# A decoder layer on one core: first channel group of two chunks, sixteen grouped blocks, x loaded first

## Chip, cores and metric

The kernel runs on one core of a Trainium2 chip. The metric is the device time of one launch in microseconds (us). Engines are TensorE (PE; PEld its weight load), VectorE (DVE), ScalarE (ACT), GpSimd (POOL), and SyncE (SP), which issues most DMAs.

## The reference, cut to what matters

One layer (256 tokens, D = 2048). A conditioning vector c gives shifts, scales and gates; the normalised x goes through one wide projection whose columns feed three token mixers and their gates; then an output projection and a SwiGLU FFN.

```
mod = silu(c) @ w_ada + b_ada
shift1, scale1, gate1, shift2, scale2, gate2 = split(mod, 6)
h = rms_norm(x, norm1_gain) * (1 + scale1) + shift1
proj = h @ w_in                      # 13840 columns: q, k, v of two attentions and a GLA, r_gla, a_gla, gates
g = sigmoid(gate_cols)               # three branches x 2048 columns, the last 6144 columns
y = g[0] * (o_sb @ w_br_sb) + g[1] * (o_dil @ w_br_dil) + g[2] * (o_gla @ w_br_gla)
x = x + gate1 * (y @ w_out)
h = rms_norm(x, norm2_gain) * (1 + scale2) + shift2
x = x + gate2 * ((silu(h @ w_gate) * (h @ w_up)) @ w_ffn_out)
```

## The kernel before

All matrix products are done on TensorE with each fp32 operand split in a high and a low part (hi, lo). `mm3` issues three products per 128-row chunk of channels, 512-column block and 128-token tile: hi x hi (L170), hi x lo of the weights (L171), lo of the activation x hi (L172). `load_weights` brings two chunks of 512 columns in one DMA into `raw` (4 buffers), ACT casts them into `whi` (L162, 4 buffers) and VectorE subtracts to get `wlo` (L163, 4 buffers). `block` runs the products of one column block over a range of chunks, for both token tiles, into two PSUM banks of the pool `acc` (4 banks).

h needs shift1 and scale1 for each of the 16 channel chunks, and these are sums over all of w_ada's rows, which have to be loaded first. So the first 13 column blocks of w_in (0 to 12) are not run over all 16 chunks at once. The chunks are cut in groups, `GROUPS` = (0 to 3), (3 to 7), (7 to 11), (11 to 16). For each group, `proj_block(g, b)` runs all 13 blocks over the chunks of that group, and between the blocks `ada_group` loads the part of w_ada for the next group and adds it up on VectorE: `ada_mac` (L295 for the first row chunk, L297 for the others), 16 row chunks per piece of at most four channel chunks. At the end of a piece the columns are summed over partitions by transposes (L347) and a reduction (L348), `finish_columns` (L354, L357) adds bias and gain, and `make_h` writes the hi part (L464, ACT), the fp32 value (L470, ACT, or L468, VectorE) and the lo part (L471, VectorE) of h.

The sum of a block over its groups lies in an SBUF tile A0 to A12. In the first group ACT copies the banks there (L508), in the next two VectorE adds the banks to it (L510), both token tiles. In the last group, `LAST`, ACT puts the sum back into PSUM first (L496, a seed), the products go on top of it, and ACT copies the result out (L508). The last block of a group goes on in the next one without leaving PSUM (`carry`).

`first_group` sets the start. SP issues c, three w_ada tiles, one pair of w_in chunks, x in four DMAs, then the other thirteen w_ada tiles. TensorE runs filler products of a constant tile (`keep_warm`, L452; `WARM` gives 22, 38 and 13) around the transposes of the small vectors (L256, L259) and the scaled transposes of x (`norm1`, L445). ACT does the exponential for silu(c) (L227), the squares of x (L422), the diagonal of row factors (L439) and the copies of the transposes (L446). The sums of the first two chunks are columns products with ones (L339), that of the third goes by transposes (L573). Then the first real product follows.

After the grouped blocks come the mixers between the last group's blocks, then the blocks for r_gla and for the gates (`gate_block`, three branches times four column blocks, each over all 16 chunks), the branch products (`y_block`), the output projection and the FFN. In the background, by `tick` at a rate per two chunks (`RATE_IN`, `RATE_MID`), the other segments of w_ada are loaded and added up by VectorE.

The order on each engine is worked out ahead by a scheduler from priorities (`prio`) and readiness; `tc.issue_after` forces an instruction behind another one.

Of the kernel before, what the change touches and what calls it, by code (L numbers as in the profile page):

```python
# [17 lines left out]
P = 128  # L18
# [14 lines left out]
RATE_IN, RATE_MID = 0.8, 0.6  # L33
# [6 lines left out]
WARM = (22, 38, 13)  # L40
FIN = 13
GROUPS = ((0, 3), (3, 7), (7, 11), (11, 16))
# [35 lines left out]
def trunk(ctx: ExitStack, tc: tile.TileContext, I, out):  # L78
# [95 lines left out]
    def block(pss, act, src, k0, k1, c0, base=0, w=None, tiles=range(NT), go_on=False, more=False, seeded=False,  # L174
              steps=None, pace=None):

        if w is None:  # L180
            w = load_weights(src, k0, k1, c0)
        if pace is None:
            pace = 1.0 if tiles[-1] == NT - 1 else 0.0
        for k in range(k0, k1):
            if (k - k0) % 2 == 0:
                tick(state["rate"] * pace)
            if k - k0 == DEFER and later:
                with tc.issue_after(state["mm"].ins), prio():
                    later.pop()()
            if steps and k - k0 in steps:  # L190
                with tc.issue_after(state["mm"].ins), prio():
                    steps[k - k0]()
            wh, wl = w[k - k0]
            for t in tiles:
                h, l = act(base + k, t)
                mm3(pss[t], h, l, wh, wl, k == k0 and not go_on, k == k1 - 1 and not more, seeded)
# [30 lines left out]
    nc.scalar.activation(ctmp, c_ps, AF.Exp, scale=-1.0)  # L227
# [75 lines left out]
    def ada_group(k0, k1, tags=ADA_TAGS, between=None):  # L303

        n = k1 - k0
        sh, sc = mod1[:, 0, k0:k1], mod1[:, 1, k0:k1]
        count = 0
# [28 lines left out]
        gains[GROUPS.index((k0, k1))] = (sh, sc)  # L336
# [78 lines left out]
    def norm1():  # L415
# [3 lines left out]
        for t in range(NT):  # L419
            for hf in range(2):  # L420
                junk = S(f"H{t}", [P, 2, NB])
                act(junk, xin[2 * t + hf], AF.Square, accum_out=part[:, hf, t : t + 1])  # L422
# [36 lines left out]
    def make_h(k, sh, sc, early=False):  # L459

        src = xT[k // 4][:, k % 4, :]
        hf = scr([P, T])
        hi = hT[0][k // 4][:, k % 4, :]
        done = nc.scalar.activation(hi, src, AF.Identity, bias=sh, scale=sc)  # L464
        state.setdefault("h_first", done)
        state["h_hi"] = done
        if early:
            nc.vector.tensor_scalar(hf, src, sc, sh, op0=ALU.mult, op1=ALU.add)  # L468
        else:
            nc.scalar.activation(hf, src, AF.Identity, bias=sh, scale=sc)  # L470
        state["h_lo"] = nc.vector.tensor_tensor(hT[1][k // 4][:, k % 4, :], hf, hi.bitcast(F32), op=ALU.subtract)  # L471
# [14 lines left out]

    def proj_block(g, b, w=None, carry=False, steps=None):
        k0, k1 = GROUPS[g]
        go_on = bool(carried)
        pss = carried.pop() if go_on else [acc_bank() for _ in range(NT)]  # L490
        seeded = g == LAST and not go_on
        if seeded:

            with prio():
                for t in range(NT):
                    nc.scalar.copy(pss[t], A[b][:, t, :])  # L496
            go_on = True
        block(pss, h_at, w_in, k0, k1, b * NB, w=w, go_on=go_on, more=carry, seeded=seeded, steps=steps)
        if carry:
            carried.append(pss)  # L500
            return
        with prio():
            first = A[b] is None
            if first:
                A[b] = S(f"A{b}", [P, NT, NB])
            for t in range(NT):
                if first or seeded:
                    nc.scalar.copy(A[b][:, t, :], pss[t])  # L508
                else:
                    nc.vector.tensor_add(A[b][:, t, :], A[b][:, t, :], pss[t])  # L510

# [10 lines left out]
    def first_group():  # L522
# [4 lines left out]
        tags = tuple(f"A{j}" for j in range(9)) + ADA_TAGS  # L527
        raws = []

        def load(ks):  # L530
            for k in ks:
                raw = S(tags[k % len(tags)], [P, 2, w])
                nc.sync.dma_start(raw, w_ada[k * P : (k + 1) * P, : 2 * D].rearrange("p (s c) -> p s c", s=2)[:, :, :w])
                raws.append(raw)
# [16 lines left out]
        for k in range(KC - 1):  # L551
            with tc.issue_after(split.ins) if k > 3 else nullcontext():
# [3 lines left out]

        def last_mac(q):
            return ada_mac(acc[:, :, chunk(q)], raws[KC - 1][:, :, chunk(q)], KC - 1)

        for q in range(n):  # L560
            last_mac(q)
        behind = state["warm"]
        for q in range(n):
            if q < 2:
                sums = misc_bank([P, 2])
                for j in range(2):
                    with tc.issue_after(behind.ins):
                        behind = column_sum(sums[:, j : j + 1], acc[:, j, chunk(q)])
            else:
                ps = misc_bank([P, 2, P])  # L570
                for j in range(2):
                    with tc.issue_after(behind.ins):
                        behind = nc.tensor.transpose(ps[:, j, :], acc[:, j, chunk(q)], ident)  # L573
                sums = small([P, 2])
                with tc.issue_after(state["h_lo"].ins):
                    nc.vector.reduce_sum(sums, ps, axis=AX.X)
            finish_columns(sums[:, 0:1], sh[:, q : q + 1], SEG_SHIFT1, q)
            finish_columns(sums[:, 1:2], sc[:, q : q + 1], SEG_SCALE1, q, ROW_N1)
            make_h(q, sh[:, q : q + 1], sc[:, q : q + 1], True)
            if q == 1:  # L580
                state["casts_after"] = state["h_hi"].ins
                with tc.issue_after(state["h_lo"].ins):
                    early.extend(load_weights(w_in, 2, n, orders[0][0] * NB, ahead=False))
# [9 lines left out]
    nc.vector.tensor_scalar(qg_sb[:, 0:1], vec[:, ROW_SBQ : ROW_SBQ + 1], rs, None, op0=ALU.mult)  # L593
    nc.vector.tensor_scalar(qg_sb[:, 1:2], vec[:, ROW_DILQ : ROW_DILQ + 1], rs, None, op0=ALU.mult)

    for g in range(len(GROUPS) - 1):
        nxt = ada_group(*GROUPS[g + 1])
        steps = KC * -(-(GROUPS[g + 1][1] - GROUPS[g + 1][0]) // 4)
        done = 0
        for n, b in enumerate(orders[g]):  # L600
            while done < (steps * n // (FIN - 1) if g == 0 else steps * (n + 1) // FIN) and next(nxt, "end") != "end":
# [4 lines left out]
            proj_block(g, b, early if (g, n) == (0, 0) else None, carry=n == 12)  # L606
        for _ in nxt:
            pass
        h_group(g + 1)

# [426 lines left out]
    ring["tags"] = ("AR0", "AR1", "KC", "OD")  # L1037

# [17 lines left out]
    gtags = (("A2", "A3", "A4"), ("A7", "A8", "T0"))  # L1056
    gates = {}

    def gate_block(n, br, steps=None):
# [3 lines left out]
        g = S(gtags[n % 2][br], [P, NT, NB])  # L1063
# [19 lines left out]
    for br in range(3):  # L1083
        nc.scalar.activation(gates[0, br], gates[0, br], AF.Sigmoid)
# [78 lines left out]
    for br in range(3):  # L1163
        gate_block(1, br)
    y_block(0)
    for br in range(3):
        gate_block(2, br)
    y_block(1)
    for br in range(3):
        gate_block(3, br)  # L1170
# [457 lines left out]
```

## Time and profile before

| | before |
|---|---|
| median of 3 runs | 1582.43 us (1582.24 to 1582.99) |
| span of the profiled execution | 1580.9 us (its own time is not given beside the span) |
| TensorE busy | 1570.4 us, 99% |
| VectorE busy | 1346.6 us, 85% |
| ScalarE busy | 856.1 us, 54% |
| DMA, mean over the span | 254 GB/s |
| granted TensorE clock | 1.000 |

The page counts an engine busy from the start to the modelled end of each instruction. The span runs from the first to the last instruction; the median of the runs lies 1.5 us above it. A timeline row gives the start, the busy time, the engine, the line, what is written from what, the shapes and the count; in square brackets stands the idle time before it and what ended it. A row of the groups gives the total busy time in us, the mean of one in ns, and the idle time before the group. A row of the windows gives, after the length, the busy time and count of PE, PEld, DVE, ACT and POOL, the granted clock, the DMA share and GB/s. A row of the waits gives the total in us, how often, and the longest.

### The profile page before, as it was taken

How to read it: one execution, taken by the hardware profiler on the slowest of the kernel's cores; microseconds unless marked ns; L12 is line 12 of the kernel's file. 1: busy time of each engine (PE TensorE's matmuls, PEld its weight loads, DVE VectorE, ACT ScalarE, POOL GpSimd, SP SyncE). 2: the span in 40 equal slices, each digit the busy share in tenths (PEclk: the TensorE clock that was granted, in tenths of full speed). 3: DMA queues.
4: the chain of work that ended last, by engine and by line, in shares of the span. 5: the costliest groups of instructions: out<-in, count | busy, mean ns of one | idle time of the engine just before them, and what ended most of it. 6: DMA issues, size and time to landing. Idle time of an engine off the chain costs nothing.

```text
span 1580.9 us, 20197 instructions
## 1 busy us (share of the span) xinstructions
PE 1570.4 (99%) x7219; PEld 1300.1 (82%) x7219; DVE 1346.6 (85%) x1632; ACT 856.1 (54%) x1186; POOL 12.6 (1%) x24
## 2 busy tenths in 40 slices
PE   8999999999999999999999999999999999999998
PEld 7878888888888888888888888888888888888887
DVE  6889996888888687877777887999999999999986
ACT  5654448875755444444445645555555555455553
POOL 1000000000000000000000000000000000000000
PEclk9999999999999999999999999999999999999999
DMA  9999987677788899889777785665566556876664
GB/s 335 350 336 323 336 301 241 219 227 224 238 280 271 293 318 321 305 273 312 269 267 245 257 299 196 211 211 190 198 200 207 195 198 218 303 236 194 222 211 147
DMA packets 196316, 402.26 MB, mean 254 GB/s; under 512 B 13102, under 2 KB 28116, under 8 KB 196216
## 3 DMA queue, kind: packets, MB, share of 16 engines
q1 hardware_dynamic: 194952, 397.75, 74.8%
q0 software_dynamic: 1088, 3.16, 0.5%
q8 instruction: 57, 0.93, 0.2%
q14 instruction: 43, 0.35, 0.1%
q10 hardware_dynamic: 176, 0.07, 0.0%
HBM read 395.68 MB, written 5.24 MB: 254 GB/s over the span
## 4 chain that ended last, share of the span: by engine, by line
PE 92%; ACT 3%; DVE 2%; DMA 1%; issue 1%; SPq 0%; ACTq 0%; DVEq 0%
PE acc L172 22%; PE acc L171 22%; PE acc L170 22%; PE misc L171 6%; PE misc L170 6%; PE misc L172 6%; DMA raw<-w_in 1%; ACT whi L162 1%; PE acc L452 1%; PE misc L821 1%; PE misc L1135 1%; DVE wlo L163 1%; DMA A<-x 0%; PE misc L445 0%; ACT A L508 0%
## 5 line engine op out<-in xcount | busy, mean ns | idle before, releaser
L162 ACT CAST whi<-raw 128x1024 fp32r<-128x1024 f32 x325 | 329.7, 1018 | 361.2 <-PE acc L172 267.6
L163 DVE TENSOR_TENSOR wlo<-raw,whi 128x1024 fp32r<-128x1024 f32 x325 | 380.5, 1178 | 142.0 <-ACT whi L162 140.7
L170 PE MATMUL acc<-whi,H 128*128 128x512 f32 x1145 | 447.8, 392 | 1.2 <-ACT H L464 0.8
L171 PE MATMUL acc<-wlo,H 128*128 128x512 f32 x1145 | 446.4, 390 | 0.8 <-DVE wlo L163 0.7
L172 PE MATMUL acc<-whi,H 128*128 128x512 f32 x1145 | 446.4, 390 | 0.5 <-DVE H L471 0.4
L172 PEld LDWEIGHTS acc<-whi,H 128*128 128x128 f32 x1145 | 214.8, 188 | 46.2 <-DVE H L471 1.6
L170 PEld LDWEIGHTS acc<-whi,H 128*128 128x128 f32 x1145 | 215.0, 188 | 45.8 <-ACT H L464 1.3
L171 PEld LDWEIGHTS acc<-wlo,H 128*128 128x128 f32 x1145 | 215.1, 188 | 44.9 <-DVE wlo L163 1.7
L1357 ACT CAST whi<-raw 128x1024 fp32r<-128x1024 f32 (+1 forms) x163 | 155.3, 968 | 112.2 <-PE acc L172 39.2
L1343 DVE TENSOR_TENSOR wlo<-raw,whi 128x1024 fp32r<-128x1024 f32 (+1 forms) x163 | 178.1, 1115 | 10.0 <-ACT whi L1357 8.9
L172 PE MATMUL acc<-whi,A 128*128 128x512 f32 x234 | 91.1, 389 | 0.0
L170 PE MATMUL acc<-whi,A 128*128 128x512 f32 x224 | 87.7, 391 | 0.0
L171 PE MATMUL acc<-wlo,A 128*128 128x512 f32 x224 | 87.2, 389 | 0.0
L170 PE MATMUL misc<-whi,H 128*128 128x512 f32 (+1 forms) x201 | 78.2, 389 | 0.0
L171 PE MATMUL misc<-wlo,H 128*128 128x512 f32 (+1 forms) x201 | 78.0, 388 | 0.0
L172 PE MATMUL misc<-whi,H 128*128 128x512 f32 (+1 forms) x201 | 77.9, 388 | 0.0
L1343 DVE TENSOR_TENSOR A<-raw,A 128x1024 fp32r<-128x1024 f32 (+2 forms) x59 | 61.2, 1049 | 5.7 <-ACT A L1357 5.3
L1357 ACT CAST A<-raw 128x1024 fp32r<-128x1024 f32 (+1 forms) x47 | 45.8, 988 | 33.5 <-PE acc L172 14.0
L297 DVE SCALAR_TENSOR_TENSOR ada<-AR,csil,ada 128x1024 f32<-128x1024 f32 x39 | 49.7, 1280 | 6.9 <-DMA AR<-w_ada 6.9
L172 PEld LDWEIGHTS acc<-whi,A 128*128 128x128 f32 x234 | 43.9, 188 | 9.2
L171 PEld LDWEIGHTS acc<-wlo,A 128*128 128x128 f32 x224 | 42.1, 188 | 8.6
L170 PEld LDWEIGHTS acc<-whi,A 128*128 128x128 f32 x224 | 42.1, 188 | 8.5
(501 smaller groups left out, 2488.7 us busy)
## 6 DMA issues: line engine op xcount, KB each, us to landing
raw<-w_in SPq DMA_DIRECT2D x205, 512.0 KB, 5.0
raw<-w_ffn_in SPq DMA_DIRECT2D x176, 512.0 KB, 4.5
raw<-w_ffn_out SPq DMA_DIRECT2D x74, 512.0 KB, 5.2
AR<-w_ada SPq DMA_DIRECT2D x58, 512.0 KB, 5.0
raw<-w_out SPq DMA_DIRECT2D x32, 512.0 KB, 5.0
OS<-w_ada SPq DMA_DIRECT2D x24, 512.0 KB, 6.4
KC<-w_ada SPq DMA_DIRECT2D x23, 512.0 KB, 5.1
KD<-w_ada SPq DMA_DIRECT2D x21, 512.0 KB, 5.5
```

The lines of the kernel that those rows point to most:

```text
L162: state["cast"] = nc.scalar.copy(hi[:, :n, :], raw[:, :n, :])
L163: state["split"] = nc.vector.tensor_tensor(lo[:, :n, :], raw[:, :n, :], hi[:, :n, :].bitcast(F32), op=ALU.subtract)
L170: nc.tensor.matmul(ps, lh, rh, start=start, stop=False, skip_group_check=seeded)
L171: nc.tensor.matmul(ps, lh, rl, start=False, stop=False, skip_group_check=seeded)
L172: state["mm"] = nc.tensor.matmul(ps, ll, rh, start=False, stop=stop, skip_group_check=seeded)
L297: nc.vector.scalar_tensor_tensor(acc, raw, c, acc, op0=ALU.mult, op1=ALU.add)
L452: state["warm"] = nc.tensor.matmul(ps, ones_r, wide, start=True, stop=True)
L821: nc.tensor.matmul(ps[:n, t * N_GLA + h, :].rearrange("p (s l) -> p s l", l=L), at(f, h, t)[:, :n], odd(at(f, h, t)), start=True, stop=True,)
L1135: nc.tensor.transpose(ps[:, i, :], src[:, i * P : (i + 1) * P], ident)
L1343: done = nc.vector.tensor_tensor(dst, x, y, op=ALU.subtract)
L1357: nc.scalar.copy(hi[:, :n, :], src)
```

## The change

The channel groups become five: (0 to 2), (2 to 5), (5 to 8), (8 to 11), (11 to 16). The blocks that run by groups become sixteen: blocks 13 to 15 are the second column block of each gate branch, which ran over all chunks as `gate_block(1, br)` before. Their sums lie in three new tiles A13 to A15, and their sigmoid is done later. Room is made by a smaller scratch for GpSimd's DMA descriptors.

In the groups in the middle the sum of the second token tile is put back into PSUM by ACT and copied out by ACT, as in the last group; that of the first tile is still added by VectorE. In the last group both tiles are put back.

At the start x is loaded before the w_ada tiles; these hold two chunks each and have tiles of their own (A0 to A7, two per tile). The first weight pair is issued behind ten of them. Its cast and the squares of x are tied behind the exponential of c. The fillers are 22, 13 and 10. The modulation sums of all later groups are one sequence, due at steps 16, 37, 58 and 80 by the end of each group. The background rate `RATE_MID` goes from 0.6 to 0.7, and the gate tiles are dealt out anew.

```diff
-RATE_IN, RATE_MID = 0.8, 0.6
+RATE_IN, RATE_MID = 0.8, 0.7
-WARM = (22, 38, 13)
-FIN = 13
-GROUPS = ((0, 3), (3, 7), (7, 11), (11, 16))
+WARM = (22, 13, 10)
+GROUPED = 16
+GROUPS = ((0, 2), (2, 5), (5, 8), (8, 11), (11, 16))
+ADA_BY = (16, 37, 58, 80)
...
-    nc.scalar.activation(ctmp, c_ps, AF.Exp, scale=-1.0)
+    c_exp = nc.scalar.activation(ctmp, c_ps, AF.Exp, scale=-1.0)
...
-                act(junk, xin[2 * t + hf], AF.Square, accum_out=part[:, hf, t : t + 1])
+                with tc.issue_after(c_exp.ins):
+                    act(junk, xin[2 * t + hf], AF.Square, accum_out=part[:, hf, t : t + 1])
...
-    A = [None] * 13
-    up, down = list(range(13)), list(range(12, -1, -1))
-    orders = (up[1:] + up[:1], up, down)
+    A = [None] * GROUPED
+    up, down = list(range(GROUPED)), list(range(GROUPED - 1, -1, -1))
+    orders = (up, down, up, down)
...
+    def column(b):
+        return b * NB if b < 13 else COL_G + (b - 13) * D + NB
...
-        pss = carried.pop() if go_on else [acc_bank() for _ in range(NT)]
-        seeded = g == LAST and not go_on
+        if go_on:
+            pss, held = carried.pop()
+        else:
+            pss = [acc_bank() for _ in range(NT)]
+            held = () if first else (0, 1) if g == LAST else (1,)
             with prio():
-                for t in range(NT):
+                for t in held:
                     nc.scalar.copy(pss[t], A[b][:, t, :])
...
-                if first or seeded:
+                if first or t in held:
                     nc.scalar.copy(A[b][:, t, :], pss[t])
                 else:
                     nc.vector.tensor_add(A[b][:, t, :], A[b][:, t, :], pss[t])
...
-        load(range(0, 3))
-        early.extend(load_weights(w_in, 0, 2, orders[0][0] * NB, ahead=False))
+        load_x()
+        load(range(0, 5))
+        state["casts_after"] = c_exp.ins
+        early.extend(load_weights(w_in, 0, n, column(orders[0][0]), ahead=False))
         split = state["split"]
-        load_x()
-        load(range(3, KC))
+        load(range(5, KC // 2))
...
-            with tc.issue_after(split.ins) if k > 3 else nullcontext():
+            with tc.issue_after(split.ins) if k >= 13 else nullcontext():
                 ada_mac(acc, raws[k], k)
...
+            with tc.issue_after(state["h_f"].ins) if q else nullcontext():
+                finish_columns(sums[:, 0:1], sh[:, q : q + 1], SEG_SHIFT1, q)
+                finish_columns(sums[:, 1:2], sc[:, q : q + 1], SEG_SCALE1, q, ROW_N1)
...
-    nc.vector.tensor_scalar(qg_sb[:, 0:1], vec[:, ROW_SBQ : ROW_SBQ + 1], rs, None, op0=ALU.mult)
+    with tc.issue_after(state["h_lo"].ins):
+        nc.vector.tensor_scalar(qg_sb[:, 0:1], vec[:, ROW_SBQ : ROW_SBQ + 1], rs, None, op0=ALU.mult)
...
+    def ada_groups():
+        for a, b in GROUPS[1:]:
+            yield from ada_group(a, b)
+    nxt, done = ada_groups(), 0
+    for g in range(LAST):
+        base = ADA_BY[g - 1] if g else 0
         for n, b in enumerate(orders[g]):
+            due = ADA_BY[0] * n // (GROUPED - 1) if g == 0 else base + (ADA_BY[g] - base) * (n + 1) // GROUPED
+            while done < due and next(nxt, "end") != "end":
                 done += 1
...
+    for b in range(13, GROUPED):
+        proj_block(LAST, b)
...
-    gtags = (("A2", "A3", "A4"), ("A7", "A8", "T0"))
-    gates = {}
+    gtags = {0: ("A2", "A3", "A4"), 2: ("A7", "A8", "T0"), 3: ("A2", "A3", "A4")}
+    gates = {(1, br): A[13 + br] for br in range(3)}
...
-    for br in range(3):
-        gate_block(1, br)
...
-    nc = _bacc.Bacc("TRN2", target_bir_lowering=False, num_devices=1)
+    nc = _bacc.Bacc("TRN2", target_bir_lowering=False, num_devices=1, dynamic_dma_scratch_size=4096)
```

More of the change, by code (lines that the diff above doesn't have):

```diff
@@ L195, in block @@
                 h, l = act(base + k, t)
-                mm3(pss[t], h, l, wh, wl, k == k0 and not go_on, k == k1 - 1 and not more, seeded)
+                mm3(pss[t], h, l, wh, wl, k == k0 and not (go_on or t in held), k == k1 - 1 and not more, seeded or t in held)
     def split_from_psum(hi, lo, ps):
@@ L306, in ada_group @@
         sh, sc = mod1[:, 0, k0:k1], mod1[:, 1, k0:k1]
+        gains[GROUPS.index((k0, k1))] = (sh, sc)
         count = 0
```

79 lines of the change are left out of this document (30 added, 49 removed).

## The prediction

> **What bounds the kernel now.** I read the page first (span, busy shares, the chain that ended last), then what TensorE waits for, then the start of the timeline.
>
> ```profile
> span 1580.9 us, 20197 instructions
> ...
> PE 1570.4 (99%) x7219; PEld 1300.1 (82%) x7219; DVE 1346.6 (85%) x1632; ACT 856.1 (54%) x1186; POOL 12.6 (1%) x24
> ...
> PE 92%; ACT 3%; DVE 2%; DMA 1%; issue 1%; SPq 0%; ACTq 0%; DVEq 0%
> ```
>
> ```profile
> PE acc L171 <- DVE wlo L163: 0.7, 1, 0.7
> PE acc L172 <- DVE H L471: 0.4, 1, 0.4
> ```
>
> The reader is to see that TensorE holds 92% of the chain and, once real work runs, waits for almost nothing: these two are the longest of its waits on VectorE. Shortening any other engine inside the span is worth nothing unless it ends one of these waits. What can be won lies where TensorE is busy with work that computes nothing, and that is the start:
>
> ```profile
> 2.71 7.43 PE L452 MATMUL acc<-H,ones_r 128*128 128x512 f32 x22
> 9.41 1.05 ACT L162 CAST whi<-raw 128x1024 fp32r<-128x1024 f32 x1 [5.97 <-DMA raw<-w_in]
> 10.37 0.18 ACT L227 ACTIVATE tiny<-misc 128x16 f32<-128x16 f32 x1
> 10.72 1.06 ACT L422 ACTIVATE H<-A 128x1024 f32<-128x1024 f32 x1 [0.17 <-DMA A<-x]
> 10.84 0.24 PE L256 MATMUL misc<-ident,H 58*128 58x58 f32 x1 [0.69 <-DMA A<-x]
> 11.09 9.12 PE L452 MATMUL acc<-H,ones_r 128*128 128x512 f32 x38
> 18.49 0.69 ACT L439 ACTIVATE H<-ident,tiny 128x128 f32<-128x128 f32 x2
> 20.05 7.31 PE L445 MATMUL misc<-H,A 128*128 128x128 f32 x64
> 27.11 3.28 PE L452 MATMUL acc<-H,ones_r 128*128 128x512 f32 x13
> 29.00 1.28 DVE L297 SCALAR_TENSOR_TENSOR ada<-A,csil,ada 128x256 f32<-128x256 f32 x3
> 30.23 0.95 PE L339 MATMUL misc<-ones_r,ada 128*128 128x1 f32 x8
> 32.25 0.50 PE L170 MATMUL acc<-whi,H 128*128 128x512 f32 x1 [0.80 <-ACT H L464]
> ```
>
> L452 is filler (22 + 38 + 13 matmuls of one constant tile). The first product with weights comes at 32.25 us. Before it stand the chain x, squares (L422), diagonal (L439), the 64 scaled transposes (L445), and beside it the modulation sums on VectorE (L297), whose last piece ends at 30.3, just as the last filler does. From 32.25 on, the time is the matmul count times its pace.
>
> **The change, part by part.**
>
> *Matmul count.* The grouped blocks do 16 x 16 chunk products instead of 13 x 16, and the three gate blocks that did the other 3 x 16 later are gone. The transposes that sum the modulation columns stay at 28 (two chunks go by the ones product, fourteen by transposes; before, two and fourteen as well). So TensorE's real work is equal; only filler goes, 73 to 45.
>
> *The start, by TensorE.* The 38 fillers took 20.05 - 11.09 = 8.96 us, 0.236 each; 25 fewer is 5.9. The 13 took 30.23 - 27.11 = 3.12, 0.24 each; 3 fewer is 0.7. Together 6.6 us, if what they cover is ready that much earlier: the diagonal at about 13.5 to 14.2 and the sums at about 23.6.
>
> *The start, by DMA.*
>
> ```profile
> 0.00:10.00 10.00, 7.47 (x23) 5.76 (x23) 0.75 (x5) 1.87 (x2) 4.26 (x13) 1.00 0.79 255
> 10.00:20.00 10.00, 9.31 (x41) 7.45 (x41) 8.60 (x14) 8.54 (x25) 0.00 (x0) 1.00 1.04 388
> ```
>
> The last column is GB/s: 2.55 MB have come by 10 us, then 0.388 MB per us; I go by 0.38, since the tiles' rows get shorter. x is 2.1 MB and now stands first, so its last quarter is there at about 9, where the first quarter came at 10.7 before. The squares to the diagonal took 10.72 to 19.2, 8.5 us, of which about 5 are the four squares; with the squares paced by x from about 5 us on, the diagonal is ready at 13.5 to 14.5. The first and second fillers (with the row transposes of 10.84 between them) end at 11.09 + 13 x 0.236 = 14.2. All that the first group needs is then x 2.1 + 16 x 0.26 (two chunks, was 0.39) + one weight pair 0.52 = 6.8 MB, there at 10 + 4.25 / 0.38 = 21.2; before it was 9.2 MB.
>
> *The start, by VectorE.* It now can begin with the first modulation tile, since c's exponential (10.37, queued behind the weight cast of 9.41) no longer waits for a weight transfer. It needs 14 steps of 512 columns, a first one, two of 256 and one weight split, by these rows of 30 to 246 us:
>
> ```profile
> L163 DVE TENSOR_TENSOR wlo<-raw,whi 128x1024 fp32r<-128x1024 f32 x70 | 84.9, 1221 | 12.2 <-ACT whi L162 11.4
> L162 ACT CAST whi<-raw 128x1024 fp32r<-128x1024 f32 x70 | 73.6, 1053 | 79.1 <-PE acc L172 60.2 <-DVE A L510 10.0 <-DMA raw<-w_in 8.8
> L510 DVE TENSOR_TENSOR A<-A,acc 128x512 f32<-128x512 f32 x48 | 31.4, 683 | 1.9 <-PE acc L172 1.8
> L508 ACT COPY A<-acc 128x512 f32<-128x512 f32 x27 | 15.9, 588 | 15.4 <-PE acc L172 14.4
> L163 DVE TENSOR_TENSOR wlo<-raw,whi 128x512 fp32r<-128x512 f32 x16 | 11.0, 686 | 1.3 <-ACT whi L162 1.3
> L162 ACT CAST whi<-raw 128x512 fp32r<-128x512 f32 x16 | 9.9, 620 | 1.9 <-issue 1.4 <-ACT scr L470 0.5
> L471 DVE TENSOR_TENSOR H<-scr,H 128x256 fp32r<-128x256 f32 x16 | 6.6, 420 | 0.7 <-ACT scr L470 0.4 <-ACT H L464 0.2
> L297 DVE SCALAR_TENSOR_TENSOR ada<-OS,csil,ada 128x768 f32<-128x768 f32 x6 | 6.1, 1014 | 0.0
> L297 DVE SCALAR_TENSOR_TENSOR ada<-OS,csil,ada 128x512 f32<-128x512 f32 x8 | 6.0, 747 | 0.0
> L348 DVE TENSOR_REDUCE tiny<-misc 128x3 f32<-128x384 f32 x2 | 1.0, 550 | 0.0
> L496 ACT COPY acc<-A 128x512 f32<-128x512 f32 x4 | 2.2, 578 | 0.0
> ```
>
> That is 0.5 + 14 x 0.75 + 2 x 0.43 (29.00's row) + 1.22 = 13.1 us; from the first tile's landing near 10 it ends at 23.1 to 24, and the last tile's landing at 21.2 with the steps behind the split gives the same. TensorE's fillers end at 23.65. I take 24.0 for the ones products, and 2.0 from them to the first product as before (30.23 to 32.25): the first product at 26.0, a gain of **6.2 us** (6.6 if TensorE sets it; 4 if the sums are 2 us late).
>
> *First group, sixteen blocks.* The pace of a real matmul:
>
> ```profile
> 39.09 0.39 PE L170 MATMUL acc<-whi,H 128*128 128x512 f32 x1
> 40.00 0.39 PE L171 MATMUL acc<-wlo,H 128*128 128x512 f32 x1
> ```
>
> Four intervals, 0.2275 us. A block of two chunks is 12 matmuls, 2.73 us; the group 43.7. Beside that, per block: ACT a cast 1.05 and two copies out 1.18, together 2.23; VectorE a split 1.22 and a modulation step 1.01, together 2.23; DMA 0.52 + 0.39 MB, 336 GB/s. All lie under the 2.73 us, and the DMA under the 348 GB/s that this stage moved before:
>
> ```profile
> 37.86:53.20 15.34, 15.34 (x70) 12.66 (x69) 13.47 (x15) 9.44 (x15) 0.00 (x0) 1.00 0.98 348
> ...
> 162.00:233.00 71.00, 71.00 (x319) 58.51 (x318) 69.56 (x91) 28.99 (x32) 0.00 (x0) 1.00 0.94 322
> ```
>
> The four weight buffers also reach four blocks ahead here (10.9 us) where a three-chunk block used two buffers (8.2 us). I charge 0; if the cover is gone, 0.1 to 0.2 us a block, up to 3 us.
>
> *Groups of three chunks.* 16 x 18 x 0.2275 = 65.5 us each. VectorE in the second: splits 16 x 1.91, 21 steps of 1.01, 14 sums 0.68, three h parts 0.42, reductions 1.1 and small ones: 64 us, 98%. The third comes to 62, the fourth to 66. Before, the third group alone asked 26 x 1.22 + 16 x 1.76 + 24 x 0.68 + 5 = 81 us of VectorE in 71 us, at 69.56 busy in its window, and TensorE did not stop: work slid into the last group. So over the four groups VectorE is less pressed than now. Half of each sum goes back through ACT: per block casts 1.67, one seed 0.58, one copy out 0.59, together 2.84 of 4.1 us. A seeded bank returns copy out, then seed, 1.2 us after its last product, and is wanted 4.1 us after that product; both casts of a block queued ahead add 1.67. Hidden, 1.2 us to spare; if that is gone, the last rival has the price.
>
> *Group switches.* Both waits of TensorE at a switch (0.7 for a split, 0.4 for h) are at the first. The chain of last step, transposes, reductions, h now has one block of 12 matmuls as cover instead of 18: 1.36 us less. With the sums earlier due on a freer DMA I charge half, **+0.7** (0 to 1.4). The later switches cost nothing before, and only one is added; their sums are due ahead except the last one's. 0, at most 1.1, what the first cost.
>
> *Later.* Blocks 13 to 15 end in the last group (five chunks, two seeds, two copies each), their sigmoids become three more ACT passes; the background rate goes from 0.6 to 0.7 steps per two chunks while nine gate blocks tick instead of twelve: about 110 steps of background against 106. x's second load waits for gate tiles that come free in the fourth output block instead of the third; it is wanted only after 96 matmuls, 22 us, of the output projection. The smaller descriptor scratch touches only GpSimd's transfers, busy 1%. Two VectorE gains move behind h. All under TensorE at 100%: 0.
>
> Sum: -6.2 + 0.7 = -5.5 on 1580.9, a span of 1575.4. The page gives the profiled execution no time but its span; the median of the runs, 1582.43, is 1.5 above, and I keep that: **1576.9**. The measurement can tell about 0.2%, 3.2 us.
>
> **The rivals.**
>
> *Short blocks eat half.* In the first group ACT, VectorE and DMA each stand above 80% of a block; a late transfer holds a cast and the copies out behind it on ACT. For it: ACT's 79.1 us of idle before casts include 8.8 for transfers. Against: no wait of TensorE between 38 and 84 us now. Price 2 to 4 us: about 1580.
>
> *TensorE idles before L445.* These are the fillers alone:
>
> ```profile
> 2.70:5.00 2.30, 2.29 (x5) 1.82 (x6) 1.00 0.89 314
> 7.00:10.00 3.00, 3.00 (x13) 2.16 (x12) 1.00 1.01 357
> ```
>
> The first five run at 0.46 us each, later ones at 0.23: a start of slow running, though the granted clock column says 1.00. With 25 fillers fewer, a late diagonal leaves TensorE idle and slow again. The slow stretch lasted between 2.3 and 4.3 us by these rows; I take 3.5. For a gap of 3.5 us and as long at half pace the loss is 3.5 + 1.75: first product at 31.2, about 1582. Against: the expected gap is under 0.5 us, and the 0.69 us gap at 10.84 cost no pace. The Trainium skill, "TensorE: Matmul & The Clock Gate", part 1, states such a return to half clock after an idle window of about 3.4 us; by it the fillers were worth their place, and the rows above agree with its two paces.
>
> *Slower: the cast ahead of the squares on ACT.* In the trace of before the weight cast sits ahead of c's exponential and the squares and holds them, though c was long there; it cost little, because the weights landed at 9.4. Now the weights come after x and ten modulation tiles, 5.2 MB in all, at about 10 + 2.67 / 0.38 = 17. The change ties cast and squares to the exponential but not to one another. If the cast is queued first, the squares begin at 18, the diagonal is ready at 26.4, the first product comes at 26.4 + 7.1 + 2.4 + 2.0 = 37.9: 5.6 later than before, about 1588. It decides if the cast stands ahead of the first square; against it, x is issued first and ten modulation tiles stand between it and the weights, so an order by readiness puts the squares first.
>
> *Slower: seeded banks come back late.* With 45 seeds in the three middle groups, each 0.4 us late (the 1.2 to spare used up, and 0.4 more) gives 18 us less the 5.5: about 1594. Against: the last group already seeds both banks at a block of 6.8 us with TensorE unbroken.
>
> **How the numbers follow.** Forecast 0.64 (own range 1574.7 to 1579.1: a gain of 6.6 with both switch waits gone, 7.7, at the low end; a gain of 4.7, sums 1.3 us later than taken, with the full 1.4 at the switch at the other). Short blocks 0.14, idle TensorE 0.04, cast first 0.08, late seeds 0.10. Faster by over 0.2% (under 1579.3): the forecast and nearly half of the short blocks, 0.70. Within: the rest of these and the idle, 0.12. Slower: 0.18. The range takes in all but the two slower rivals: 1574.7 to 1582.4.
>
> **What would show it.** Right: first product near 26; the squares starting near 5; 45 fillers; TensorE's waits after 26 under 2 us in sum, the largest at the first switch near 70. Wrong: a cast ahead of the first L422; waits of L170 for the seed's line; TensorE under 99% between 30 and 270 us.

## The result, and the profile after

| | before | after |
|---|---|---|
| median (runs) | 1582.71 us (1582.24 to 1584.50, 4) | 1596.17 us (1595.30 to 1596.89, 4) |
| span of the profiled execution | 1580.9 us | 1595.1 us |
| granted TensorE clock | 1.000 | 0.995 |

The changed kernel is slower: ratio 1.0084, interval [1.0070, 1.0099], 13.5 us. The forecast was 1576.9. First the page of the changed kernel: span, TensorE's share, the chain that ended last.

```profile
span 1595.1 us, 20403 instructions
...
PE 1570.7 (98%) x7191; PEld 1300.4 (82%) x7191; DVE 1349.9 (85%) x1663; ACT 927.9 (58%) x1323; POOL 13.2 (1%) x24
...
PE 85%; DVE 5%; DMA 4%; ACT 3%; issue 2%; SPq 0%; DVEq 0%; ACTq 0%
```

TensorE holds 85% of the chain where it held 92%; VectorE 5% where it held 2%, transfers 4% where they held 1%. It now waits, as its list of waits says (in total, times, longest):

```profile
PE misc L348 <- DVE ada L298: 8.2, 3, 3.7
PE misc L666 <- DVE A L654: 3.1, 1, 3.1
...
PE acc L172 <- DVE wlo L164: 1.7, 3, 0.7
PE misc L447 <- ACT T L448: 1.4, 1, 1.4
PE misc L447 <- ACT H L441: 1.2, 1, 1.2
```

L348 are the transposes that sum a group's modulation columns; they wait for VectorE's last modulation step L298. L666 are the transposes ("turns" below) of q and k of the dilated branch. Before, the longest wait on VectorE was 0.7 us.

To find where the time went I mark three points: the first product, the first transpose of the GLA mixer's output, just ahead of the branch products (L1106 here; "the branch sums" below), and the first transpose of the second norm (L1212). From the first product to the branch sums the sixteen-block kernels do 3 x 16 x 6 matmuls more than before, 65.5 us at 0.2275, and as many fewer afterwards. Beyond that, "lost" below:

| | first product | lost up to the branch sums | lost from there to the second norm |
|---|---|---|---|
| before | 32.25 | 0 (457.0 us in all) | 0 |
| after | 28.39 | 16.8 | 1.5 |

After the second norm the two differ by less than 0.3 us. So 3.9 us are won at the start, 16.8 lost up to the branch sums and 1.5 behind them: 14.4, of a span 14.2 longer. Of the 16.8, 12.1 lie ahead of the first turn of q and k (326.8).

The start, from the changed kernel's timeline:

```profile
8.91 1.06 ACT L424 ACTIVATE H<-A 128x1024 f32<-128x1024 f32 x1 [1.84 <-DMA A<-x]
...
15.03 0.70 ACT L441 ACTIVATE H<-ident,tiny 128x128 f32<-128x128 f32 x2
15.49 3.84 PE L447 MATMUL misc<-H,A 128*128 128x128 f32 x32 [1.21 <-ACT H L441]
19.11 1.04 ACT L163 CAST whi<-raw 128x1024 fp32r<-128x1024 f32 x1 [3.38 <-DMA raw<-w_in]
20.06 2.53 ACT L448 COPY T<-misc 128x512 f32<-128x512 f32 x5
20.69 3.84 PE L447 MATMUL misc<-H,A 128*128 128x128 f32 x32 [1.36 <-ACT T L448]
24.28 2.57 PE L454 MATMUL acc<-H,ones_r 128*128 128x512 f32 x10
26.69 0.95 PE L340 MATMUL misc<-ones_r,ada 128*128 128x1 f32 x8
28.39 0.50 PE L171 MATMUL acc<-whi,H 128*128 128x512 f32 x1 [0.75 <-ACT H L466]
```

ScalarE's queue holds the weight cast (19.11) ahead of the copies of the transposes (20.06); it waited 3.38 us for the weights, and TensorE then 1.36 us for a copy. The grouped stage, a row for the first group and one for each of the three behind it (PE, PEld, DVE, ACT, POOL, granted clock, DMA share, GB/s):

```profile
28.00:72.00 44.00, 43.61 (x195) 35.91 (x196) 37.30 (x48) 34.55 (x51) 0.00 (x0) 1.00 0.93 329
72.00:138.00 66.00, 65.88 (x293) 54.06 (x292) 60.20 (x79) 47.13 (x75) 0.00 (x0) 1.00 0.94 318
138.00:205.00 67.00, 61.89 (x268) 49.97 (x268) 57.30 (x84) 39.71 (x61) 0.00 (x0) 0.97 0.92 303
205.00:272.00 67.00, 62.60 (x272) 51.28 (x271) 51.91 (x68) 42.59 (x69) 1.84 (x1) 0.97 0.87 291
```

In the last two rows TensorE idles 5.1 and 4.4 us, the granted clock drops to 0.97, and VectorE is less busy, not more. One of the waits in TensorE's timeline:

```profile
195.48 0.39 PE L172 MATMUL acc<-wlo,H 128*128 128x512 f32 x1
198.44 1.09 PE L348 MATMUL misc<-ident,ada 128*128 128x128 f32 x4 [2.56 <-DVE ada L298]
199.18 0.78 PE L173 MATMUL acc<-whi,H 128*128 128x512 f32 x1
199.75 0.63 PE L171 MATMUL acc<-whi,H 128*128 128x512 f32 x1
200.18 0.63 PE L172 MATMUL acc<-wlo,H 128*128 128x512 f32 x1
...
202.22 0.40 PE L172 MATMUL acc<-wlo,H 128*128 128x512 f32 x1
202.46 0.39 PE L173 MATMUL acc<-whi,H 128*128 128x512 f32 x1
```

The products behind the transposes did not pass them. After 2.56 us of idling the matmuls start 0.43 us apart, from 199.75 to 201.5, instead of 0.23; the granted clock of that stretch is 0.50. What VectorE, and below it ScalarE, waited for between 70 and 272 us:

```profile
DVE ada L298 <- DMA OS<-w_ada: 9.0, 6, 2.4
DVE ada L298 <- DMA T<-w_ada: 6.6, 5, 2.2
...
DVE ada L298 <- DMA OD<-w_ada: 2.2, 2, 1.5
```

```profile
ACT whi L163 <- DMA raw<-w_in: 20.0, 12, 2.9
ACT acc L503 <- DVE A L515: 16.7, 15, 3.3
```

VectorE waits 17.8 us for w_ada tiles. ScalarE's seeds (L503) wait 16.7 us for VectorE's adds (L515): in the program's order the seed takes its bank before the block's first product, and the bank that is next in turn is mostly one that VectorE, not ScalarE, empties.

Three theories came from this. **S**: seeds hold ScalarE, its casts come late. **L**: the modulation loads come late. **P**: the summing transposes stand too early in TensorE's queue. A fourth question followed: whether it is the groups of three chunks at all.

### The profile page after: what moved, and what is told of

It is laid out like the page before. It is cut to its first block, busy times and chain, and to the rows that moved or that the text cites. A ratio compares the mean times of both kernels' runs of the same rounds, so it can differ in the third digit from the quotient of the medians.

```text
span 1595.1 us, 20403 instructions
## 1 busy us (share of the span) xinstructions
PE 1570.7 (98%) x7191; PEld 1300.4 (82%) x7191; DVE 1349.9 (85%) x1663; ACT 927.9 (58%) x1323; POOL 13.2 (1%) x24
## 4 chain that ended last, share of the span: by engine, by line
PE 85%; DVE 5%; DMA 4%; ACT 3%; issue 2%; SPq 0%; DVEq 0%; ACTq 0%
PE acc L173 20%; PE acc L172 20%; PE acc L171 20%; PE misc L172 6%; PE misc L171 6%; PE misc L173 6%; DMA OS<-w_ada 2%; DVE wlo L164 2%; ACT whi L163 1%; DVE ada L298 1%; PE misc L820 1%; DMA T<-w_ada 1%; PE misc L1137 1%; PE misc L348 0%; DVE A L515 0%
## 5 line engine op out<-in xcount | busy, mean ns | idle before, releaser
L163 ACT CAST whi<-raw 128x1024 fp32r<-128x1024 f32 (+1 forms) x344 | 333.2, 971 | 282.9 <-PE acc L173 174.8
L164 DVE TENSOR_TENSOR wlo<-raw,whi 128x1024 fp32r<-128x1024 f32 (+1 forms) x344 | 383.7, 1123 | 118.6 <-ACT whi L163 117.7
L1357 ACT CAST whi<-raw 128x1024 fp32r<-128x1024 f32 (+1 forms) x163 | 155.2, 968 | 112.6 <-PE acc L173 37.4
L1343 DVE TENSOR_TENSOR wlo<-raw,whi 128x1024 fp32r<-128x1024 f32 (+1 forms) x163 | 178.0, 1115 | 10.0 <-ACT whi L1357 8.8
L513 ACT COPY A<-acc 128x512 f32<-128x512 f32 x107 | 61.8, 582 | 20.0 <-PE acc L173 18.2
L503 ACT COPY acc<-A 128x512 f32<-128x512 f32 x75 | 43.9, 594 | 16.8 <-DVE A L515 16.7
L173 PEld LDWEIGHTS acc<-whi,A 128*128 128x128 f32 x234 | 44.0, 188 | 9.1
L298 DVE SCALAR_TENSOR_TENSOR ada<-AR,csil,ada 128x1024 f32<-128x1024 f32 x39 | 49.5, 1281 | 2.0 <-DMA AR<-w_ada 1.9
```

The source lines that it names most:

```text
L163: state["cast"] = nc.scalar.copy(hi[:, :n, :], raw[:, :n, :])
L164: state["split"] = nc.vector.tensor_tensor(lo[:, :n, :], raw[:, :n, :], hi[:, :n, :].bitcast(F32), op=ALU.subtract)
L173: state["mm"] = nc.tensor.matmul(ps, ll, rh, start=False, stop=stop, skip_group_check=seeded)
L298: nc.vector.scalar_tensor_tensor(acc, raw, c, acc, op0=ALU.mult, op1=ALU.add)
L1343: done = nc.vector.tensor_tensor(dst, x, y, op=ALU.subtract)
L1357: nc.scalar.copy(hi[:, :n, :], src)
```

## The experiments

Medians of the kernel before lay between 1582.7 and 1583.4 beside them; ratios are to it. A loss read from a trace is that of one execution, and the executions of one and the same kernel differ by 6.5 us in experiments 5 and 7 and by 9.6 in experiment 2. The profiled one lay above its kernel's median by 6.1 us in experiment 2, 4.8 in 5 and 2.5 in 7, and 3.3 below it in 8; the conclusions on time go by the medians.

**1. No seeds in the middle groups.**

```
- held = () if first else (0, 1) if g == LAST else (1,)
+ held = (0, 1) if g == LAST and not first else ()
```

> The changed kernel, but no sum is put back into PSUM in the groups in the middle: VectorE adds both token tiles there, as before the change. Theory S (the seeds cost the time: ScalarE holds the next casts while a seed waits for its bank) expects the three waits of the summing transposes (8.2 us) to go and about 1585 us. Theory L (the modulation loads come late, because three-chunk groups leave the weight buffers half empty and SP's queue stands behind them) expects VectorE, with 45 x 0.68 = 31 us more to do, to be later still: 1596 to 1605 us.

Measured 1593.53 us, ratio 1.0071 [1.0055, 1.0088]; lost up to the branch sums 13.4. The largest waits of TensorE:

```profile
PE acc L171 <- ACT whi L163: 4.0, 3, 1.8
PE misc L666 <- DVE A L654: 3.1, 1, 3.1
PE acc L173 <- DVE H L473: 2.6, 1, 2.6
```

The wait of the transposes is all but gone (0.2 us), and others have its place. Seeds alone are not the cause.

**2. The later groups' modulation loads issued by GpSimd.**

```
- nc.sync.dma_start(      # in ada_group
+ nc.gpsimd.dma_start(
```

> The changed kernel, with the modulation loads of the later groups issued by GpSimd's queue instead of SP's, so that they no longer stand behind weight loads. Theory L expects VectorE's waits for w_ada (17.8 us between 70 and 260 us) to fall under 5 us, the waits of the summing transposes to go, and about 1585 us. Theory S expects the seeds' waits (16.7 us of ScalarE) and the time to stay, 1593 us or more.

Measured 1607.67 us, ratio 1.0158 [1.0135, 1.0182]. The first product came at 44.24, because the loads now stood in GpSimd's queue ahead of work that the start needs. Where the loads had their effect it can still be read:

```profile
PE misc L257 <- DMA A<-w_ada: 9.2, 1, 9.2
PE misc L348 <- DVE ada L298: 8.5, 3, 3.7
PE misc L225 <- POOL ident masks.py:199: 6.4, 1, 6.4
```

VectorE's waits for w_ada in the middle groups fell from 17.8 us to none, and the transposes still waited 8.5 us; lost up to the branch sums 15.2 instead of 16.8. Theory L falls: late loads were not what the transposes waited for in the end. The seeds' wait for VectorE nearly went as well, from 16.7 to 2.4 us:

```profile
ACT acc L503 <- DVE A L515: 2.4, 4, 0.9
```

So in this trace the transposes wait as long with hardly any seed late. VectorE waits instead for ScalarE's casts (15.3 us) and for the products whose sums it adds (15.2).

**3. The accumulators in two pairs of banks**, so that a block's banks come round in turn by pairs.

```
- return psa.tile(shape or [P, NB], F32, tag="acc", name=nm("acc"))
+ acc_turn[0] += 1
+ half = acc_turn[0] % 2
+ return psa.tile(shape or [P, NB], F32, tag=f"acc{half}", name=nm("acc"), bufs=2)
```

> The changed kernel, with the four accumulator banks dealt out as two pairs, so that a seed goes into a bank that ScalarE itself emptied and not into one that VectorE's add frees. Theory S, in the form that the bank's owner is the trouble, expects ScalarE's waits for VectorE's add (16.7 us) to go and about 1586 us. Theory L expects those waits to go as well but the modulation loads to be as late as now: 1593 to 1597 us.

Measured 1590.06 us, ratio 1.0042 [1.0027, 1.0057]: 6.1 us less than the changed kernel. The seeds' wait for VectorE is gone from ScalarE's list, and the transposes' wait is halved:

```profile
PE misc L352 <- DVE ada L302: 4.2, 2, 2.3
PE misc L670 <- DVE A L658: 3.1, 1, 3.1
```

So pairs of banks, in which a seed no longer waits for VectorE, are worth 6.1 us here, although leaving the seeds out gave only 2.6: then VectorE does the adds. The edit holds for the whole kernel; 8.1 us are lost up to the branch sums here instead of 16.8, so most of what it gives lies there.

**4. The kernel before, with half of each sum put back in its middle groups.** The edit is the change's own `held`, on four-chunk groups and thirteen blocks.

> The kernel before, with one part of the change alone: in its two middle groups (four chunks each) the second token tile's sum is put back into PSUM. Theory S expects it slower than the kernel before by 3 to 10 us. Theory L expects no difference beyond 2 us, since the groups still fill the weight buffers.

Measured 1583.01 us, ratio 0.9999 [0.9990, 1.0009]. Half of the sums put back neither costs nor brings anything with groups of four.

**5. The summing transposes held behind the last product.**

```
- turned_sums(sums[:, j, :], acc[:, j, :])
+ turned_sums(sums[:, j, :], acc[:, j, :], state["mm"].ins)
```

> The changed kernel, with the summing transposes of the second and later modulation blocks held behind the last product recorded when VectorE's last modulation step is recorded, so that they can't stand earlier in TensorE's queue. Theory P (the transposes stand too early in TensorE's in-order queue and wait for VectorE's last step, three times, 8.2 us, with some 3 us at half the clock behind two of the waits): that wait goes, the stretch from the first product to the first turn of q and k falls from 298.4 us to 288-291, and the whole to 1585-1589. Theory L (VectorE is late because the modulation loads are late, whatever TensorE's order): TensorE then waits for the finished modulation or for the next group's weights instead, the stretch stays at 294 or above and the whole at 1592-1596. Theory S (ScalarE is held by seeds): the wait moves to the weights' high parts, products waiting for ScalarE 4 us or more, as when the middle seeds were left out.

Measured 1589.46 us, ratio 1.0043 [1.0028, 1.0058]: 6.7 us less than the changed kernel, lost up to the branch sums 9.9. TensorE's largest waits:

```profile
PE misc L666 <- DVE A L654: 3.1, 1, 3.1
PE acc L173 <- DVE H L473: 2.5, 3, 1.2
...
PE acc L172 <- DVE wlo L164: 1.4, 3, 0.5
```

No L348 is left. And with TensorE moving on, VectorE's waits for w_ada fell from 17.8 to 6.1 us and the seeds' from 16.7 to 7.8 in the same stretch: both had partly been consequences of the stall. Theory P holds for 6.7 us, just short of what it promised: 1585 to 1589 for the whole, and 288 to 291 us up to the first turn of q and k, which took 291.7. The edit also has a price: behind the first group, where the changed kernel waited for nothing, TensorE now waits 0.56, 0.53 and 1.15 us (74.11 to 78.18).

**6. The first cast behind the copies of the transposes.** The load of the first weights, with its cast, and the loads of the last three w_ada tiles are recorded after norm1's copies, and the modulation steps are no longer tied behind the split.

```
- state["casts_after"] = c_exp.ins
+ state["casts_after"] = state["turned"].ins    # recorded behind norm1(), with the early load
- with tc.issue_after(split.ins) if k >= 13 else nullcontext():
```

> The changed kernel, with the early load and cast of the first weights recorded behind the last copy of the input's transposes, and the late half of the first modulation block no longer tied to the split. If the cast in ScalarE's queue ahead of those copies is what cost the start 2.3 us of its forecast 6.2, the first product comes at 26.0-27.0 (28.39 in the changed kernel) and the whole at 1594-1595, 1.4-2.4 us less. If the first product waits for the modulation's VectorE steps or for their loads anyway, it stays at 28-29 and the whole at 1596.

Measured 1595.82 us, ratio 1.0078 [1.0061, 1.0096]. The first product came at 26.75, 1.6 us sooner, the median of the whole only 0.3 us. The four executions lie between 1592.98 and 1598.99, so whether the 1.6 us arrive at the end in three-chunk groups is not shown.

**7. Groups of 2, 4, 4 and 6 chunks.** With one group less, the due steps of the modulation sums and the order of the blocks in the first group are set to fit; all else is as changed.

```
- GROUPS = ((0, 2), (2, 5), (5, 8), (8, 11), (11, 16)); ADA_BY = (16, 37, 58, 80)
+ GROUPS = ((0, 2), (2, 6), (6, 10), (10, 16)); ADA_BY = (16, 38, 64)
- orders = (up, down, up, down)
+ orders = (up[1:] + up[:1], up, down)
```

> The changed kernel with its first group of two chunks, its start and its seeds, but the other fourteen chunks in groups of 4, 4 and 6, again sixteen blocks in the first three groups. If the groups of three chunks are what lost the time (more column changes, weights and modulation loads that arrive for three chunks' work), the stretches lose nothing beside the smaller groups' blocks, and the whole is 1578-1583. If the short first group or its start is what throws the modulation out of step, it stays at 1588 or more.

Measured 1582.00 us, ratio 0.9996 [0.9986, 1.0005]: 14.2 us less than the changed kernel. Lost up to the branch sums 1.5 instead of 16.8. TensorE's longest wait for a sum and ScalarE's for VectorE's adds, in its profile:

```profile
PE misc L348 <- DVE ada L298: 1.7, 1, 1.7
```

```profile
ACT acc L503 <- DVE A L515: 1.3, 1, 1.3
```

The same seeds for each block, the same sixteen blocks, the same first group of two chunks: with this grouping nearly all of the loss up to the branch sums is gone, the wait of L666 too. What is shown is the price of the grouping as a whole: groups of three against four, one group more, a last group of five against six, and the due steps that go with them. The start's 3.7 us do not show in the median, 1.3 below the kernel before; the profiled execution loses 4.1 us between the branch sums and the second norm.

**8. The background rate back to 0.6.**

```
- RATE_IN, RATE_MID = 0.8, 0.7
+ RATE_IN, RATE_MID = 0.8, 0.6
```

> The changed kernel with the background rate of the middle groups back at 0.6. The first turn of q and k waits 3.1 us for VectorE's multiplication, which stands behind five modulation steps in VectorE's queue; half the clock for some 3 us follows. If the rate 0.7 put them there, that wait goes and the whole falls by 3-5 us, to 1591-1593. If the rate is idle there, nothing changes (1595-1597); if the lower rate makes the modulation later in the groups of three chunks, the waits of the summing transposes grow and the whole is 1598 or more.

Measured 1596.13 us, ratio 1.0076 [1.0061, 1.0091]; the wait of L666 was 4.0 us in its profile. The rate is not the cause.

**9. Three-chunk groups with edits 3, 5 and 6 together.**

> The changed kernel with its three-chunk groups and three edits together: the accumulators in two pairs of banks, the summing transposes held behind the last product, the first cast behind the copies of the input's transposes. Alone they gave 6.1, 6.7 and 0.3 us. If seeds and early transposes are two causes, the sum is 13 us and the whole 1582-1585. If the two edits mend one and the same delay (ScalarE held by a seed makes VectorE late, and VectorE's lateness is what the transposes wait for), together they give little more than one of them, and the whole is 1587-1590.

Measured 1588.21 us, ratio 1.0031 [1.0019, 1.0043]. Together they give 8.0 us, where the sum of the three is 13.1: the mends overlap, as the second case expected. That the seeds are what makes the transposes wait is not shown by it; experiment 2 speaks against it. Lost up to the branch sums 8.2, with 3.1 us of waiting before the turns of the dilated branch (L669 here) and 3.9 us for parts of h and of the weights, most of it where a group begins.

**10. Four-chunk groups (7) with edits 5 and 6.**

> The four-chunk version (1582.0) with the transposes held behind the last product and the first cast behind the copies. One wait of a summing transpose is left there, 1.7 us, and the first product comes 1.6-1.9 us sooner. If the start's gain is kept, 1578.5-1580.5; if it is lost again later, as it was in the three-chunk version with the cast moved (0.3 us of 1.6 kept), 1580.5-1582.

Measured 1579.03 us, ratio 0.9976 [0.9967, 0.9986]: **faster than both kernels**, by 0.24% against the one before. The chain on its page, and the start in its timeline:

```profile
PE 93%; DVE 3%; DMA 2%; ACT 1%; issue 1%; SPq 0%; ACTq 0%; DVEq 0%
```

```profile
20.14 4.82 DVE L298 SCALAR_TENSOR_TENSOR ada<-A,csil,ada 128x512 f32<-128x512 f32 x7 [1.07 <-DMA A<-w_ada]
...
22.95 2.57 PE L454 MATMUL acc<-H,ones_r 128*128 128x512 f32 x10
25.36 0.95 PE L340 MATMUL misc<-ones_r,ada 128*128 128x1 f32 x8
27.16 0.50 PE L171 MATMUL acc<-whi,H 128*128 128x512 f32 x1 [0.86 <-ACT H L466]
```

The first product is 5.1 us sooner than in the kernel before, the median 4.3 us lower. Most of what the start wins now arrives; 3.0 us are lost behind the branch sums, where TensorE's longest wait for a cast stands at 631 us:

```profile
PE acc L171 <- ACT whi L163: 2.3, 2, 1.8
```

**11. The same with the banks in pairs (3).**

> As the last, with the accumulators in two pairs of banks. Where seeds wait for VectorE's sums, this gives something: in three-chunk groups it gave 6.1 us. If four-chunk groups leave VectorE enough ahead, no difference from the last one (within 1 us); if pairs of banks only take away freedom, 1-2 us slower.

Measured 1580.36 us, ratio 0.9982 [0.9974, 0.9991]: 1.3 us above 10, with overlapping intervals. Pairs of banks bring nothing that shows where seeds hardly wait.

**12. As 10, without seeds in the middle groups (1).**

> As the four-chunk version with both mends, but with nothing put back into PSUM in the middle groups, so that VectorE adds both halves. The seeds take some 16 adds off VectorE in each of two groups, and cost ScalarE as many copies. In the kernel before, adding them changed nothing (0.9999). If VectorE has room here too, the same time as with seeds, within 1 us; if the sixteen blocks press VectorE, 2-5 us slower.

Measured 1579.37 us, ratio 0.9978 [0.9970, 0.9987]: no difference from 10. With four chunks, putting half of the sums back is worth nothing that shows at either number of blocks.

**13. The changed kernel, the dilated q and k ahead of the waiting work, their turns later.**

```
- qk_norm(dil_parts)
+ with prio():
+     qk_norm(dil_parts)
- 7: ... qk_turn(dil_parts[:2]   10: ... qk_turn(dil_parts[2:]   13: dil_scores(0, 3)
+ 12: ... qk_turn(dil_parts[:2]  13: ... qk_turn(dil_parts[2:]   14: dil_scores(0, 3)
```

> The changed kernel, with the squares, the root and the multiplications of the dilated branch's q and k recorded ahead of the waiting work (they passed five background modulation steps on VectorE and two casts on ScalarE), and their turns five chunks of the next block later. If the 3.1 us wait of these turns and the half clock behind it are all that the changed kernel loses between the first turn of q and k and the gated branch sums (some 4.5 us), the wait goes and the whole falls by 4-5 us, to 1591-1592. If VectorE or ScalarE is late there as a whole, another wait takes its place within 20 us and the whole stays at 1595 or more.

Measured 1599.49 us, ratio 1.0098 [1.0082, 1.0113], no better than the changed kernel. The wait of L666 is gone and another has its place, 14 us earlier:

```profile
PE misc L348 <- DVE ada L298: 7.8, 4, 2.8
PE acc L171 <- ACT whi L163: 5.4, 2, 4.2
```

The squares of q and k now stand ahead of ScalarE's casts (461.2 to 468.2 us), and a product waits 4.2 us for one. The second outcome held: freeing this turn alone wins nothing.

**14. Three-chunk groups with edits 3, 5, 6 and 13.**

> The three-chunk version with three mends (1588.2) and this fourth one. If the waits at the group changes (4.2 us by the profile) and this turn (4 us) are what three chunks still lose, 1583.5-1585: level with the kernel before, and 4-5 us behind the four-chunk version with the mends (1579.0). If it stays at 1587-1589, the turn costs nothing by itself.

Measured 1589.99 us, ratio 1.0038 [1.0026, 1.0051]: not better than 9. Its longest wait is again the 4.2 us for a cast. With the same three mends, three-chunk groups (9) stay 7.9 us behind four-chunk groups (11).

## Why the prediction was wrong, step by step

*The start* was forecast at 26.0, a gain of 6.2, and measured 28.39, a gain of 3.9. The fillers went as counted (45), the squares began at 5.9, the diagonal was there at 15.7, 1.2 us behind the late end of its forecast, because x's second quarter came only at 8.9. What failed here is the dismissal of the ScalarE rival, which was too narrow: the cast did not stand ahead of the squares, but it stood ahead of the copies of the transposes, and waited 3.38 us for its weights there. With the cast behind them (6, 10) the first product came at 26.75 and 27.16, 0.8 to 1.2 later than even the forecast's 26.0. There the late diagonal sets the time: in 10 the transposes of x began at 15.79 instead of 14.2 and the last filler ended at about 25.4 instead of 23.65, with the ones products (25.36) right behind it; VectorE's sums, ended at 25.0 (20.14 and 4.82) instead of 24.0, were late too, but done before.

*First group, sixteen short blocks*, charged nothing: right. TensorE is busy for 43.61 of the 44 us to 72, where 43.7 were counted, and the four-chunk version keeps this group and loses 1.5 us up to the branch sums.

*Groups of three chunks* is the step that made the prediction wrong: "over the four groups VectorE is less pressed than now" was true and beside the point. I added up each engine's work per group against TensorE's time. VectorE was indeed less busy, 60.2, 57.3 and 51.9 us of 66 to 67; it lost its time waiting, and TensorE lost its own in a queue in which the transposes stood ahead of products that were ready. Sums of work don't show that. Experiment 7 shows the price: 14.2 us for this grouping against the one with four chunks, with the start, the first group, the kind of seeds and the sixteen blocks as they were. Of this 6 to 8 us go with the mends of the transposes and the banks (3, 5, 9). For the rest, 7.9 us between 9 and 11 with the same mends, no cause is shown.

*Seeds*: "A seeded bank returns copy out, then seed" failed: in the middle groups the bank that the seed takes is mostly freed by VectorE's add. The rival "seeded banks come back late" named the right engines and, by chance of its price, nearly the right time, 1594. But its form was another: no product waits for a seed in the list of TensorE's waits. The seed waits on ScalarE, 16.7 us in 15 times, and casts stand behind it. And a cost of the seeds shows only with three chunks (3 against 4 and 12).

*Group switches*, +0.7: the wrong place was priced. At the first switch TensorE waits for nothing in the changed kernel; with four chunks in the second group it waits 2.2 us there (7). "Their sums are due ahead except the last one's" took it that sums due early cost nothing, and the last one's at most 1.1. The three waits of L348, at 165, 198 and 250 us, are two such sums and the last one, all inside the groups, at blocks of 4.1 us where they had 5.5 before, and cost 2.0, 2.6 and 3.7 us.

*The rival that TensorE runs slow after idling* was priced for the start; it came true in the middle, where no wait was forecast: part of what the waits of 2.56, 3.11 and 3.71 us cost was the half pace behind them.

*Later*, charged nothing: wrong by the 4.7 us lost between the first turn of q and k and the branch sums (16.8 less 12.1), with the wait of L666 and the slow pace behind it, and 1.5 further on. Why the last group is late in each of the three-chunk versions is not settled: not the rate (8), not the order of these steps alone (13, 14). What exactly in three chunks makes VectorE and ScalarE late (weights in half-size loads, shorter blocks as cover, the one group more, or the steps at which the sums are due) was not separated either.

*The rest of the forecast*, that only filler can be won and that sixteen blocks are neutral, agrees with 10: its median is 4.3 us lower with a start 5.1 us shorter, and the 1576.9 lie 2.1 us below what the four-chunk version with two mends reached (1579.03).

## What to carry to other kernels

A group's work per engine can fit well and the group still be slow: for each step that one engine finishes for another, ask where the receiving instruction stands in its in-order queue, and what ready work is stuck behind it. Before a buffer is counted as free, find which engine empties the one that is next in turn. And when a start is shortened, change the stage behind it as little as can be: here the shorter first group paid with four chunks in the later groups and two mends, and lost with three.

## What the runs showed of the hardware that was not expected

TensorE dropped to half pace after shorter idling than I had priced, and not each time. In the changed kernel the matmuls came 0.43 us apart for some 2 us after gaps of 2.56 us (198.44) and 3.71 us (249.55), at a granted clock of 0.50; after 1.96 us (165.41) they came at 0.23 at once. In experiment 8 a gap of 2.57 us at the same transposes was followed by 0.23 and a clock of 1.00:

```profile
199.35 0.63 PE L348 MATMUL misc<-ident,ada 128*128 128x128 f32 x4 [2.57 <-DVE ada L298]
```

In experiment 5 gaps of 0.56, 0.53 and 1.15 us within 5 us were enough; from 79.28 to 82.3 the pace is half and the clock 0.50:

```profile
76.31 0.72 PE L172 MATMUL acc<-wlo,H 128*128 128x512 f32 x2 [0.53 <-DVE wlo L164]
78.18 0.73 PE L173 MATMUL acc<-whi,H 128*128 128x512 f32 x2 [1.15 <-DVE H L473]
...
79.28 0.63 PE L173 MATMUL acc<-whi,H 128*128 128x512 f32 x1
79.70 0.63 PE L171 MATMUL acc<-whi,H 128*128 128x512 f32 x1
```

Two short gaps do not always do it either: 1.29 and 0.53 us in experiment 7 (634.99) did, 1.76 and 0.52 us in experiment 10 (631.30) did not. So neither the length of one gap nor the sum of two decides by itself. Nor do the transposes that follow a gap: a gap of 2.12 us with none (experiment 6, 648.78) brought the clock to 0.50, one of 2.54 us with six (experiment 2, 76.89) left the pace at 0.23. What does decide is not shown. The Trainium skill, "TensorE: Matmul & The Clock Gate", part 1, gives in its table one idle window of about 3.4 us as the condition. The gap of 3.71 us agrees with it; the gap of 2.12 us and the short ones of experiments 5 and 7 differ from it, and they decide here.
